# A sliding-window copy by DMA alone: what is staged in SBUF, and how the rest is cut

## The chip, the cores and the metric

The kernel runs on one core of one Trainium2 chip. The metric is the device time of one execution in microseconds; the times given are medians of several runs. The profile is of one more execution, and its span, from the first to the last recorded instruction, lies a little under the timed value.

## What is computed

The reference cuts each of 32 sequences into overlapping windows. It is a pure copy:

```python
x: float32 [32, 4096, 256];  window_size = 64;  stride = 32
n_windows = (4096 - 64) // 32 + 1            # 127
for i in range(n_windows):
    result[:, i] = x[:, i * 32 : i * 32 + 64]
```

With a stride of half a window, each sequence ("batch") is 128 **blocks** of 32 rows, 32 KiB each. Window w is block w followed by block w + 1. So each block but the first and the last of a batch is written twice: as the first half (half 0) of window w, and as the second half (half 1) of window w - 1. The output has 32 x 127 x 2 = 8128 halves of 32 KiB, 266.3 MB; the input has 134.2 MB.

## The kernel before

There are two ways for a block to get to its two places. **Direct**: a DMA from HBM to HBM, which reads the block once for each place. **Staged**: one DMA loads the block into SBUF, two DMAs store it from there. A direct block moves two blocks' worth of bytes through the DMA engines, a staged one three; but a direct block reads HBM twice, a staged one once. The kernel mixes both. SyncE's queue carries the direct copies, ScalarE's the staging, GpSimd's the windows that lie between a staged and a direct batch.

The helpers that name the copies:

```python
DIRECT, IN, OUT = 32768, 16384, 16384        # longest piece of a row, bytes

def windows(self, q, b, w0, n, half=None, piece=DIRECT):
    # n windows of batch b from w0: whole (64 KiB rows) or one half of each (32 KiB rows)
    row = [1, 2 * blk if half is None else blk]
    ...out=self.oap(..., [[2 * blk, n], row]), in_=self.xap(..., [[blk, n], row])...

def load(self, q, t, b, c, rows):            # SBUF tile [128, block] <- blocks, one a partition
def store(self, q, t, b, c, rows, half):     # one half of n windows <- tile
```

Eleven batches of 32 are staged whole, 128 blocks to a tile, in groups of 6 tiles: six loads, twelve stores, and the same for the other five. A load waits for the stores that last used its tile; a store waits for its load.

```python
staged = [*range(1, B, 3)]
items = [(b, -1 if b == B - 1 else 0, c.nb) for b in staged]
...
for g in group: self.load(q, g)      # one DMA of 128 rows (the very first in 4 parts)
for g in group: self.store(q, g)     # two DMAs of 128 rows: half 0, half 1
```

A whole batch of blocks stored at both halves puts one half before the batch's first window and one after its last; these belong to the neighbouring batches, and are written over later.

The direct copies are 16 windows a DMA, either as one DMA of whole windows or as two of halves. How often they are halved depends on what the staging ring is thought to be doing then (`share`):

```python
share += 120 if turns < 16 or -8 <= second < 16 else 90 if loading else 18
if share >= 120:
    share -= 120; turns += 4
    count(c.windows(ring_d, b, w, 16, 0), done)
    count(c.windows(ring_d, b, w, 16, 1), sem)
else:
    turns += 3
    count(c.windows(ring_d, b, w, 16), sem)
```

What 16 doesn't divide, and the windows that staged batches wrote over, come at the end on GpSimd's queue, 15 windows a DMA:

```python
ring_r.wait_ge(near, 16)             # the second-last of the direct copies
for b, w, n in edges:                # wait for the neighbours' stores, then
    count(c.windows(ring_r, b, w, n), rest)
count(c.columns(ring_r, last, 116, 9), rest)     # the last windows in small pieces
st.wait_stored(ring_d, place[B - 1])
count(c.columns(ring_d, last, 125, 2), done)
```

Of the kernel before, what the change touches and what calls it, by code (L numbers as in the profile page):

```python
# [8 lines left out]
DIRECT, IN, OUT = 32768, 16384, 16384  # L9


class Copier:


    def __init__(self, x, out, B, L, D, W, S, n_win):
        assert W == 2 * S and L % S == 0
        self.x, self.out = x, out
        self.B = B
        self.blk = S * D
        self.nb = L // S  # L20
        self.nw = n_win

    def xap(self, block, dims):
        return bass.AP(self.x.tensor, self.x.offset + block * self.blk, dims)

    def oap(self, half_window, dims):
        return bass.AP(self.out.tensor, self.out.offset + half_window * self.blk, dims)

    def windows(self, q, b, w0, n, half=None, piece=DIRECT):

        blk = self.blk
        row = [1, 2 * blk if half is None else blk]
        h = half or 0
        return q.dma_start(  # L34
            out=self.oap((b * self.nw + w0) * 2 + h, [[2 * blk, n], row]),
            in_=self.xap(b * self.nb + w0 + h, [[blk, n], row]),
            max_dma_last_dim=piece,
        )

    def columns(self, q, b, w0, n):  # L40

        part = self.blk // 8
        row = [1, part]
        return q.dma_start(  # L44
            out=self.oap((b * self.nw + w0) * 2, [[part, 16], [2 * self.blk, n], row]),
            in_=self.xap(b * self.nb + w0, [[part, 16], [self.blk, n], row]),
        )

    def load(self, q, t, b, c, rows):

        p, step, n, unit = rows
        return q.dma_start(
            out=t[p : p + (n - 1) * step + 1 : step, :],
            in_=self.xap(b * self.nb + c + p // unit, [[step // unit * self.blk, n], [1, self.blk]]),
            max_dma_last_dim=IN,
        )

    def store(self, q, t, b, c, rows, half):


        p, step, n, unit = rows
        w = b * self.nw + c + p // unit - half
        return q.dma_start(
            out=self.oap(2 * w + half, [[2 * step // unit * self.blk, n], [1, self.blk]]),
            in_=t[p : p + (n - 1) * step + 1 : step, :],
            max_dma_last_dim=OUT,
        )


class Staging:  # L70


    def __init__(self, c, tc, pool, dtype, items, bufs):
        self.c, self.items = c, items
        self.tiles = [pool.tile([128, c.blk], dtype, name=f"xb{i}") for i in range(bufs)]
        self.loaded = [tc.alloc_semaphore(f"loaded{i}") for i in range(bufs)]
        self.stored = [tc.alloc_semaphore(f"stored{i}") for i in range(bufs)]
        self.ended = tc.alloc_semaphore("ended")
        self.count = {sem: 0 for sem in (*self.loaded, *self.stored, self.ended)}
        self.after_load, self.after_store = {}, {}  # L80

    def issue(self, dma, sem):
        dma.then_inc(sem, 16)
# [1 line left out]

    def load(self, q, g):
        i = g % len(self.tiles)
        b, c, n = self.items[g]
        if self.count[self.stored[i]]:
            q.wait_ge(self.stored[i], self.count[self.stored[i]])  # L90
        step = 128 // n
        parts = [(k, 4, 32, 1) for k in range(4)] if g == 0 else [(0, step, n, step)]
        for rows in parts:
            self.issue(self.c.load(q, self.tiles[i], b, c, rows), self.loaded[i])
        self.after_load[g] = self.count[self.loaded[i]]

    def store(self, q, g):
        i = g % len(self.tiles)
        b, c, n = self.items[g]
        q.wait_ge(self.loaded[i], self.after_load[g])  # L100
        step = 128 // n
        parts, end = [((0, step, n, step), 0), ((0, step, n, step), 1)], []
        if g == len(self.items) - 1:

            parts = [((0, 1, 128, 1), 1), ((0, 1, 32, 1), 0)]
            end = [(96, 1, 32, 1)] + [(32 + k, 4, 16, 1) for k in range(4)]
        for rows, half in parts:
            self.issue(self.c.store(q, self.tiles[i], b, c, rows, half), self.stored[i])
        for rows in end:
            self.issue(self.c.store(q, self.tiles[i], b, c, rows, 0), self.ended)  # L110
        self.after_store[g] = self.count[self.stored[i]]

    def wait_stored(self, q, g):
        q.wait_ge(self.stored[g % len(self.tiles)], self.after_store[g])  # L114

    def run(self, q):
        bufs = len(self.tiles)
        for first in range(0, len(self.items), bufs):
            group = range(first, min(first + bufs, len(self.items)))
            for g in group:  # L120
                self.load(q, g)
            for g in group:
                self.store(q, g)


@with_exitstack
def kernel(
    ctx: ExitStack,
    tc: tile.TileContext,
    x: bass.AP,  # L130
    window_size: bass.AP,
    stride: bass.AP,
    out: bass.AP,
):
    nc = tc.nc
    W, S = int(window_size), int(stride)
    B, L, D = x.shape
    n_win = (L - W) // S + 1
    assert out.shape == (B, n_win, W, D)
    c = Copier(x, out, B, L, D, W, S, n_win)  # L140


    staged = [*range(1, B, 3)]
    items = [(b, -1 if b == B - 1 else 0, c.nb) for b in staged]
    place = {b: g for g, (b, _, n) in enumerate(items) if n == c.nb}
    direct = [b for b in range(B) if b not in staged]
    pool = ctx.enter_context(tc.tile_pool(name="xb", bufs=1))
    st = Staging(c, tc, pool, x.dtype, items, 6)
    ring_d, ring_s, ring_r = nc.sync, nc.scalar, nc.gpsimd
    done = tc.alloc_semaphore("done")  # L150
    near = tc.alloc_semaphore("near")
    rest = tc.alloc_semaphore("rest")
    total = {done: 0, near: 0, rest: 0}

    def count(dma, sem):
        dma.then_inc(sem, 16)
        total[sem] += 16

    sixteens = []
    for b in direct:
        w = 15 if b - 1 in staged else 0
        sixteens += [(b, w + 16 * j) for j in range((c.nw - w) // 16)]
    singles = [(B - 1, c.nw - 1, 1)]
    edges = [(b, 0 if b - 1 in staged else 112, 15) for b in direct[:-1]]
    last = B - 2
    edges.append((last, 112, 4))

    first_loads, loads, stores = 6 * 17, 5 * 17, 6 * 34  # L170
    turns = share = 0
    with tc.tile_critical():  # L172
        st.run(ring_s)

        for i, (b, w) in enumerate(sixteens):
            sem = near if i == len(sixteens) - 2 else done
            second = turns - first_loads - stores
            loading = turns < first_loads or 0 <= second < loads
            share += 120 if turns < 16 or -8 <= second < 16 else 90 if loading else 18
            if share >= 120:  # L180
                share -= 120
                turns += 4
                count(c.windows(ring_d, b, w, 16, 0), done)
                count(c.windows(ring_d, b, w, 16, 1), sem)
            else:
                turns += 3
                count(c.windows(ring_d, b, w, 16), sem)
            if i == len(sixteens) // 2:
                for b, w, half in singles:
                    count(c.windows(ring_d, b, w, 1, half, 2048), done)  # L190

        ring_r.wait_ge(near, 16)
        for b, w, n in edges:
            for k in (b - 1, b + 1):
                if k in place and b != last:
                    st.wait_stored(ring_r, place[k])
            count(c.windows(ring_r, b, w, n), rest)


        count(c.columns(ring_r, last, 116, 9), rest)  # L200
        st.wait_stored(ring_d, place[B - 1])
        count(c.columns(ring_d, last, 125, 2), done)
        total[st.ended] = st.count[st.ended]
        for sem, n in total.items():
            ring_d.wait_ge(sem, n)


# [33 lines left out]
```

## Time and profile before

| | |
|---|---|
| time, median of 3 runs | 755.48 us (754.17 to 756.32) |
| span of the profiled execution | 749.4 us |
| bytes through the DMA engines | 313.26 MB, mean 418 GB/s |
| busy engines | GpSimd 12.8 us, for issuing; no other |
| DMAs on SyncE, ScalarE, GpSimd | 204, 41, 22 |

The page's line of tenths shows how busy the core's 16 DMA engines are in 40 equal slices of the span, and the line under it the GB/s they moved. A queue's line has its packets, their bytes, and the time they took as a share of 16 engines' span. A direct copy is counted once in the bytes, though HBM is both read and written; HBM's own traffic stands in a line of its own. Packets under 512 B are those that count up a semaphore at a DMA's end, one on each engine. Sizes of DMAs, and how long one took from issue to landing (the median), are in the last part of the page:

| DMAs | count | KB each | us to landing |
|---|---|---|---|
| direct, whole windows (SyncE) | 92 | 1024 | 100.7 |
| direct, halves (SyncE) | 110 | 512 | 90.3 |
| loads (ScalarE) | 10 | 4096 | 131.4 |
| edges (GpSimd) | 20 | 960 | 38.5 |

A load or a store of a whole tile is 128 rows of 32 KiB, 4096 KB. Landing times are long because the queues are deep.

### The profile page before, as it was taken

The numbers are of one execution on the slowest core, as the hardware profiler recorded it, in microseconds if no ns is written. First come the engines' busy times: TensorE is split into PE (matmuls) and PEld (weight loads), VectorE is DVE, ScalarE is ACT, GpSimd is POOL, SyncE is SP. The second block draws the span as 40 slices with busy tenths as digits, with TensorE's granted clock in tenths as the row PEclk, the third lists the DMA queues.
The fourth block names the chain that finished last, engine by engine and source line by source line (L and its number), as shares of the span: only waits on it lengthen the run. The fifth ranks groups of instructions, "written<-read, shape, count | busy, mean of one in ns | idle before, by whom it ended". The sixth has DMA issues, their size and how long they took to land.

```text
span 749.4 us, 322 instructions
## 1 busy us (share of the span) xinstructions
POOL 12.8 (2%) x26
## 2 busy tenths in 40 slices
POOL 0000000000000000000000000000000000040100
DMA  8999999999999999999999999999999999999996
GB/s 360 401 427 429 427 429 428 434 423 418 420 424 423 418 424 415 422 427 427 414 427 417 429 432 429 430 422 430 429 423 421 423 421 419 425 426 423 431 409 262
DMA packets 18290, 313.26 MB, mean 418 GB/s; under 512 B 4336, under 2 KB 4336, under 8 KB 4528
## 3 DMA queue, kind: packets, MB, share of 16 engines
q1 hardware_dynamic: 8016, 154.32, 48.8%
q10 hardware_dynamic: 9104, 138.41, 44.0%
q0 software_dynamic: 1168, 20.51, 6.5%
q14 instruction: 2, 0.02, 0.0%
HBM read 220.95 MB, written 267.09 MB: 651 GB/s over the span
## 4 chain that ended last, share of the span: by engine, by line
another core or an unknown queue 92%; POOL 2%; issue 0%; POOLq 0%; SPq 0%
POOL out_dram L34 2%; POOL out_dram L44 0%; POOLq L236 0%; SPq L172 0%; POOLq L114 0%
## 5 line engine op out<-in xcount | busy, mean ns | idle before, releaser
L34 POOL DMA_DIRECT2D out_dram<-in_x_dram x21 | 12.0, 576 | 691.3 <-DMA out_dram<-in_x_dram 654.0
L44 POOL DMA_DIRECT2D out_dram<-in_x_dram x1 | 0.6, 581 | 0.0
L222 POOL MEMSET const-float32-0.0<- 128x1 f32 x1 | 0.1, 98 | 0.2 <-issue 0.2
L222 POOL MEMSET const-bfloat16-1.0<- 128x1 bf16 x1 | 0.1, 101 | 0.0
L222 POOL MEMSET const-float32-1.0<- 128x1 f32 x1 | 0.1, 98 | 0.0
L222 POOL MEMSET const-uint8-127<- 128x1 uint8 x1 | 0.1, 98 | 0.0
## 6 DMA issues: line engine op xcount, KB each, us to landing
out_dram<-in_x_dram SPq DMA_DIRECT2D x92, 1024.0 KB, 100.7
out_dram<-xb ACTq DMA_DIRECT2D x21, 4096.0 KB, 139.7
out_dram<-in_x_dram SPq DMA_DIRECT2D x110, 512.0 KB, 90.3
xb<-in_x_dram ACTq DMA_DIRECT2D x10, 4096.0 KB, 131.4
out_dram<-in_x_dram POOLq DMA_DIRECT2D x20, 960.0 KB, 38.5
xb<-in_x_dram ACTq DMA_DIRECT2D x4, 1024.0 KB, 15.7
out_dram<-xb ACTq DMA_DIRECT2D x2, 1024.0 KB, 113.4
out_dram<-xb ACTq DMA_DIRECT2D x4, 512.0 KB, 96.9
```

What stands on the lines that cost most here:

```text
L34: return q.dma_start(out=self.oap((b * self.nw + w0) * 2 + h, [[2 * blk, n], row]), in_=self.xap(b * self.nb + w0 + h, [[blk, n], row]), m ...
L44: return q.dma_start(out=self.oap((b * self.nw + w0) * 2, [[part, 16], [2 * self.blk, n], row]), in_=self.xap(b * self.nb + w0, [[part, 16 ...
L222: nc = _bacc.Bacc("TRN2", target_bir_lowering=False, num_devices=1)
```

## The change

It changes what is staged. Instead of all 128 blocks of 11 batches, the inner blocks 1 to 64 of 23 batches are: each of them belongs in two windows of its own batch, so nothing is stored outside its place. Two batches, 16 apart, share a tile: one has the even partitions, the other the odd ones; each has its own load and its own two stores of 64 rows. Batch 11 has a tile alone.

```diff
-    staged = [*range(1, B, 3)]
-    items = [(b, -1 if b == B - 1 else 0, c.nb) for b in staged]
+    far, pairs, n = B // 2, 11, 64
+    items = [(g, far, 1, n) for g in range(pairs + 1)]
+    alone = pairs
```

```diff
-        step = 128 // n
-        parts = [(k, 4, 32, 1) for k in range(4)] if g == 0 else [(0, step, n, step)]
+        step = 4 if g == 0 else 2
+        for k in range(step if g != self.alone else 1):
+            dma = self.c.load(q, self.tiles[i], b + far * (k % 2), c + k // 2, k, step, 2 * n // step)
```

```diff
+        for half in (0, 1):
+            for k in (0, 1) if g != self.alone else (0,):
+                self.issue(self.c.store(q, self.tiles[i], b + far * k, c, k, n, half), self.stored[i])
```

The direct copies follow from it. Windows 65 to 112 of every batch go 16 a DMA (`whole`). The nine batches that aren't staged have their blocks 1 to 64 copied as halves (`split`). Windows 113 to 126 don't make a sixteen; these are gathered **across** 16 batches, one window of each in a DMA, so the rows read lie a whole batch (4 MiB) apart. The same goes for the two halves that border on the staged part (half 0 of window 0, half 1 of window 64).

```diff
+    def across(self, q, b, w, half=None):
+            out=self.oap(b, w, h, [[2 * self.nw * blk, 16], row]),
+            in_=self.xap(b, w + h, [[self.nb * blk, 16], row]),
...
+    for b in range(B):
+        whole += [(b, w) for w in range(n + 1, n + 49, 16)]
+        if b % far >= pairs and b != alone:
+            split += [(b, w) for w in range(0, n, 16)]
+    for w in range(n + 49, n_win):
+        cross += [(b, w) for b in (0, far)]
+    where = len(whole) // 4
+    jobs = whole[:where] + cross + whole[where:]          # shortened
```

The balance between the rings is set anew, with many more halves; a halved turn takes a split pair first, while there are any:

```diff
-    first_loads, loads, stores = 6 * 17, 5 * 17, 6 * 34
+    first_loads, loads, stores = 6 * 18, 5 * 18 + 9, 6 * 36
...
-            share += 120 if turns < 16 or -8 <= second < 16 else 90 if loading else 18
+            share += 120 if turns < 16 or -8 <= second < 16 else 106 if loading else 95
```

GpSimd's queue, the edges, the small pieces at the end (`columns`) and the waits for neighbours' stores are gone; SyncE waits for its own copies and for all stores.

```diff
-        ring_r.wait_ge(near, 16)
-        for b, w, n in edges:
-            ...
-        count(c.columns(ring_r, last, 116, 9), rest)
-        st.wait_stored(ring_d, place[B - 1])
-        count(c.columns(ring_d, last, 125, 2), done)
+        ring_d.wait_ge(done, total)
+        st.wait_all(ring_d)
```

## The prediction

> **What bounds the kernel now.** No engine computes; all is transfers. So the first view to read is the page's second and third parts: how busy the 16 DMA engines are, and what each queue moved.
>
> ```profile
> DMA  8999999999999999999999999999999999999996
> GB/s 360 401 427 429 427 429 428 434 423 418 420 424 423 418 424 415 422 427 427 414 427 417 429 432 429 430 422 430 429 423 421 423 421 419 425 426 423 431 409 262
> DMA packets 18290, 313.26 MB, mean 418 GB/s; under 512 B 4336, under 2 KB 4336, under 8 KB 4528
> ...
> q1 hardware_dynamic: 8016, 154.32, 48.8%
> q10 hardware_dynamic: 9104, 138.41, 44.0%
> q0 software_dynamic: 1168, 20.51, 6.5%
> ...
> HBM read 220.95 MB, written 267.09 MB: 651 GB/s over the span
> ```
>
> The DMA engines are full in every slice but the first and the last. q1 is SyncE's ring (direct copies, 32 KiB pieces), q10 ScalarE's (staging, 16 KiB pieces), q0 GpSimd's (the edges). There is no gap to close in the middle, so the time is bytes through the engines divided by a rate, plus what is lost at the two ends. The second view, the table of stretches, shows that this rate isn't one number:
>
> ```profile
> 0.00:20.00 20.00, 0.20 (x4) 1.00 0.90 367
> 20.00:40.00 20.00, 0.00 (x0) 1.00 1.00 401
> ...
> 200.00:300.00 100.00, 0.00 (x0) 1.00 1.01 421
> ...
> 440.00:540.00 100.00, 0.00 (x0) 1.00 1.01 429
> 560.00:640.00 80.00, 0.00 (x0) 1.00 1.01 423
> 660.00:740.00 80.00, 6.95 (x13) 1.00 1.01 421
> 740.00:749.00 9.00, 0.00 (x0) 1.00 0.31 127
> ```
>
> The last column is GB/s, the one before it the DMA engines' busy share. The rate moves between 421 and 429 with the engines equally full. The third view, the queues in two of these stretches, says with what it moves. From 200 to 300 us, then from 440 to 540 us:
>
> ```profile
> q1 hardware_dynamic: 1173, 24.18, 57.6%
> q10 hardware_dynamic: 1176, 17.96, 42.9%
> ```
>
> ```profile
> q1 hardware_dynamic: 1275, 23.30, 54.5%
> q10 hardware_dynamic: 1274, 19.56, 46.1%
> ```
>
> A direct byte crosses HBM twice, a staged one once. In the first stretch 24.18 / 42.14 MB = 57.4% of the bytes are direct, at 421 GB/s; in the second 23.30 / 42.86 = 54.4%, at 429 GB/s. From 560 to 640 us it is again 57% (19.40 of 33.81 MB), at 423. In HBM traffic that is 421 x 1.574 = 663 GB/s against 429 x 1.544 = 662: about the same. So I read two limits that lie close together: the engines' own rate (near 430) and HBM's (near 663), and a mix with more direct bytes falls to the second. The waits view confirms that nothing but ring ends is waited for: GpSimd's 654 us are the wait, by design, for the second-last direct copy.
>
> ```profile
> POOL out_dram L34 <- DMA out_dram<-in_x_dram: 654.0, 1, 654.0
> POOL out_dram L34 <- DMA out_dram<-xb: 37.4, 1, 37.4
> ```
>
> **What the Trainium skill says.** (1) "DMA: Bandwidth & Descriptors", section "Where 436 GB/s comes from": 16 ports of 32 B at 850 MHz make 435 GB/s. The trace agrees: its best long stretch has 429. (2) The same page, "Queues, rings and completion order": each engine takes the queue rows it has work for in turn, a packet of each. The trace agrees closely: 1173 to 1176 packets and 1275 to 1274 in the stretches above. So a ring's share of the bytes follows from its packets' sizes, the 4-byte semaphore packets counting as turns too. (3) "HBM Reference", "Specifications (TRN2)": about 716 GB/s for the domain. 663 GB/s is 93% of that, near enough to call it a limit that is felt. (4) The first page again, "Latency and other measured facts": copies whose rows lie 4 MiB apart in both tensors ran at half rate (103 against 214 GB/s a direction), rows 512 KiB apart at full rate. No stretch of this trace has such a pitch; the change brings one.
>
> **The change, part by part.**
>
> *Bytes.* Staged loads: before 11 batches x 128 blocks = 1408 blocks, after 23 x 64 = 1472. Blocks are 32 KiB, so loads go from 46.14 to 48.23 MB, +2.10 MB. The halves that whole-batch staging stored outside their place (one at each end of 11 batches, 22 of 32 KiB, 0.72 MB) go. After: the output's 8128 window halves of 32 KiB, 266.34 MB, plus 48.23 MB of loads make 314.57 MB, against 313.26 on the page. At the mean middle rate of before, 424 GB/s, +1.31 MB is **+3.1 us**.
>
> *The mix.* Of the 8128 halves 2944 come from the staging tiles, 5184 are direct: 169.87 MB, 54.0% of 314.57. Before it was 154.32 + 20.51 = 174.83 MB, 55.8%. And the changed schedule spreads it evenly: SyncE's DMAs are nearly all halves (two packets for 32 KiB) throughout, where before the loading stretches had many halves and the storing stretches few. From the instruction order, 28 whole copies and 268 halves remain, 324 data and 296 semaphore packets an engine, 620 turns. Staging makes 552 data packets and 71 semaphores, 623 turns. Taking turns, both rings run from start to end, and every stretch should have 53 to 56% direct, like the stretch at 429. I take 428.5 GB/s: 314.57 MB / 428.5 = 734.1 us. Before, the middle from 40 to 740 us ran at 424 (313.26 less 7.34, 8.02 and 1.14 MB in 700 us); at that rate the new bytes would take 741.9. The mix is thus worth **-7.8 us**. As a cross-check, packet times from the 440 to 540 stretch: 46.1% of 1600 us over 1194 packets of 16 KiB is 0.618 us, 54.5% over 711 of 32 KiB is 1.226 us. 552 x 0.618 + 324 x 1.226 = 738 engine-us, and as the shares there add to 1.006, 734 us of time.
>
> *The ends.* The first 40 us moved 15.36 MB instead of 17.1 at 428.5, a loss of 4.1 us. The new start (the same four-part first tile, the same halves) keeps it. The last 9.4 us moved 1.14 MB, a loss of 6.7 us. Of that, the part owed to GpSimd's late edges, 15 windows on 16 engines, may go; but the 16 engines still finish apart, and the small columns that evened them out are gone as well. I keep 6.5.
>
> *More DMAs.* 267 become 367 (71 on ScalarE, 296 on SyncE, none on GpSimd), so 100 more 4-byte packets an engine. The stretch with most of them (644 of 2549) is the fastest, so I take 0 to 1 us: 0.5. Issue is no limit: SyncE's shortest took 0.57 us, 296 x 0.57 = 169 us.
>
> *Across 16 batches.* 28 copies of 1 MiB and 4 of 512 KiB read rows 4 MiB apart, one row on each engine; by the turns they run at about 275 to 400 us. The skill's slow case has 128 rows, so on 16 engines of 8 consecutive rows the engines stand 8 pitches apart (an estimate from that page): 32 MiB where it was slow, 4 MiB where the 512 KiB pitch was fast. Here engines stand 4 MiB apart, and only the reads. I charge 2 us.
>
> *Half-tile staging DMAs.* Loads and stores now take every second partition, 64 rows. The first tile's parts (32 rows, every fourth partition) did already: from 3 to 8 us q10 had 1.03 MB at 52.7%, 42 us over 63 packets, 0.67 us each, at a cold start, against 0.618. No cost is charged.
>
> Sum: 734.1 + 4.1 + 6.5 + 0.5 + 2 = 747.2 us of span, against 749.4. The timed median lies 6.1 above the span before (755.48); with the same added, **753 us**.
>
> **Rivals.** *Only bytes count*: if the engines' 424 is a fixed mean and the mix tells nothing, the time is 755.5 + 3 = 758 to 759. For it: engines are equally "full" at 421 and 429. Against: the rate follows the direct share in three stretches. *HBM rows collide*: if the 4 MiB pitch halves the cross copies' rate, their 60 to 62 packets of 1.23 us an engine take 75 us more, about 825; a tenth of that effect gives 760. Against it: engines drift apart, and the other ring's packets lie between; no row of before can show it. *The rings come apart*: if one ring ends early, the other runs alone; were it the direct one, all its bytes would cross HBM twice and 663 / 2 = 331 GB/s remain, so 10 us of overhang cost about 3. The turns (620 and 623) speak against more. *The end shrinks*: without GpSimd's edges the tail could lose 3 us less, giving 750.
>
> **Range and chances.** 753 is the sum; 745 needs the mix, no pitch cost and a better end; 764 holds the bytes-only case with some pitch cost. Over 2% faster would be under 740.4, which needs the engines' best rate in every stretch and no lost ends: 4%. Over 2% slower is above 770.6, the pitch rival at a fifth of its size or more: 9%. Within 2%: 87%.
>
> **What would show it.** Right: about 314.6 MB, HBM read 218 MB, no q0; stretches from 40 to 730 us at 427 to 430 with 53 to 56% direct; q1 and q10 both busy to the last 10 us. Wrong: a dip of GB/s between 275 and 400 us with full engines (the pitch); 424 at 54% direct (the mix tells nothing); q10 packets above 0.63 us (the half tiles); a last stretch with one queue alone. The pitch is what would make it most wrong.

## The result and the profile after

The changed kernel took **812.28 us** (median of 6 runs, 810.13 to 815.88), against 755.66 for the kernel before in the same set: 1.0754 times as long, 95% interval 1.0725 to 1.0782. The prediction had 753, within 745 to 764.

The page of the changed kernel, the lines that answer to those shown of before:

```profile
DMA  8999999999999999999999999999999999999996
GB/s 363 422 425 410 432 430 424 432 430 426 428 422 426 374 269 287 297 283 265 293 291 276 319 429 428 401 426 424 431 429 428 420 426 425 427 422 429 421 424 292
DMA packets 19891, 314.62 MB, mean 388 GB/s; under 512 B 5872, under 2 KB 5872, under 8 KB 5872
...
q1 hardware_dynamic: 9920, 169.89, 53.9%
q10 hardware_dynamic: 9968, 144.71, 45.6%
...
HBM read 218.10 MB, written 266.34 MB: 597 GB/s over the span
```

The bytes are as counted, and the DMA engines are "busy" throughout. The row of tenths alone would show nothing wrong. The row under it does: from the 14th slice to the 23rd the rate is about a third lower, and on both sides of that it is the old one. The table of stretches (busy share of the DMA engines, then GB/s, at the end of each line; the last line is the clean stretch behind the dip):

```profile
200.00:250.00 50.00, 0.00 (x0) 1.00 1.00 425
250.00:300.00 50.00, 0.00 (x0) 1.00 1.02 356
300.00:350.00 50.00, 0.00 (x0) 1.00 1.00 285
350.00:400.00 50.00, 0.00 (x0) 1.00 1.01 285
400.00:450.00 50.00, 0.00 (x0) 1.00 1.00 283
450.00:500.00 50.00, 0.00 (x0) 1.00 1.01 395
...
550.00:790.00 240.00, 0.00 (x0) 1.00 1.01 426
```

That is where the copies across 16 batches run. The five stretches from 250 to 500 us moved 50 us x (356 + 285 + 285 + 283 + 395) = 80.2 MB, which takes 188 us at the 426 GB/s of the stretch from 550 to 790 us: **62 us** are lost there. Without them the span of 811.5 would be about 749.5.

How the loss looks to each queue: SyncE's (q1) and ScalarE's (q10), first from 300 to 450 us, then from 600 to 700 us, each line with packets, MB and the share of 16 engines' time:

```profile
q1 hardware_dynamic: 1348, 23.14, 54.7%
q10 hardware_dynamic: 1347, 19.48, 45.8%
```

```profile
q1 hardware_dynamic: 1332, 23.10, 54.6%
q10 hardware_dynamic: 1333, 19.37, 45.9%
```

The packets, the MB and the shares are nearly equal; only the stretches differ, 150 us and 100. A direct piece of 32 KiB took 54.7% x 2400 us / 706 = 1.86 us instead of 54.6% x 1600 / 705 = 1.24. And a staged piece of 16 KiB, which has nothing to do with the across copies but runs on the same engines and HBM, took 0.92 instead of 0.62. Of the across copies an engine has 56 pieces, and by the ratio of the stretch (706 to 1189) some 94 staged ones beside them: 56 x 0.62 + 94 x 0.30 = 63 us, the loss again.

### The profile page after: what moved, and what is told of

The parts are those of the page before. It is cut to its first block, busy times and chain, and to the rows that moved or that the text cites. A ratio compares the mean times of both kernels' runs of the same rounds, so it can differ in the third digit from the quotient of the medians.

```text
span 811.5 us, 420 instructions
## 1 busy us (share of the span) xinstructions
POOL 0.2 (0%) x4
## 2 busy tenths in 40 slices
DMA packets 19891, 314.62 MB, mean 388 GB/s; under 512 B 5872, under 2 KB 5872, under 8 KB 5872
## 3 DMA queue, kind: packets, MB, share of 16 engines
HBM read 218.10 MB, written 266.34 MB: 597 GB/s over the span
```

## The experiments

The sets below ran on different chips; the kernel before took 745 to 756 us on them, so each ratio is against the kernel before on the same chip, and rates in GB/s are best compared within a run or on one chip. Theory A is that rows a multiple of 4 MiB apart, read by 16 engines at once, are slow. Theory B is that gathering from 16 far batches is slow whatever the pitch, or that the far writes are.

### Another pitch for the reads alone

```diff
-            in_=self.xap(b, w + h, [[self.nb * blk, 16], row]),
+            in_=self.xap(b, w + h - 15, [[(self.nb + 1) * blk, 16], row]) if w > self.nb // 2
+            else self.xap(b, w + h, [[self.nb * blk, 16], row]),
```

> The across copies read rows 4 MiB + 32 KiB apart instead of 4 MiB (so they read other blocks than the reference asks for); the writes, sizes, counts and order are as in the changed kernel. Theory A (the reads' exact 4 MiB pitch slows them): the dip of 283 to 285 GB/s goes, every stretch has 425 to 430, and the time falls from 812 to 747 to 755 us. Theory B (writes 127 windows apart, or gathering from 16 batches at whatever pitch): the dip stays, about 812 us. If the pitch were only part of it, something between.

752.33 us, 1.0012 times the kernel before (0.9997 to 1.0026). The across copies' stretch, then the clean one after it, from the table of stretches of this run:

```profile
280.00:410.00 130.00, 0.00 (x0) 1.00 1.01 415
480.00:730.00 250.00, 0.00 (x0) 1.00 1.01 429
```

415 instead of 285: the reads' pitch is what costs. The same far batches, writes and counts are there, so theory B falls. The remaining 14 GB/s over 130 us are 4 us. The rate was expected at 425 or more, so the time came out as theory A had it and the stretch a little short. (This kernel copies other blocks to windows 113 to 126 than the reference asks for; so do the next two and the last one.)

### Four pitches in one run

```diff
+    for i, pitch in enumerate([4194304, 2097152, 1048576, 524288]):
+        jobs += [("whole", *k) for k in whole[24 * i : 24 * i + 12]]
+        jobs += [(pitch // 4, *k) for k in cross[7 * i : 7 * i + 7]]
+        jobs += [("whole", *k) for k in whole[24 * i + 12 : 24 * i + 24]]
```

> The 28 across copies in four groups of 7, apart from each other in the order, with reads at a pitch of 4 MiB, 2 MiB, 1 MiB and 512 KiB (other blocks than the reference asks for; same writes). Theory A: the first group dips to about 285 GB/s for some 45 us, the second to between 285 and 428, the last two not below 420; the time is about 812 - 63 x 3/4 + a part for 2 MiB, 765 to 785 us. Theory B: four equal dips, about 812 us in all.

771.7 us, one run. Each group's stretch was found from its copies' issue and their 88 us to landing. The table of stretches, 4 MiB, 2 MiB, 1 MiB and 512 KiB in order:

```profile
240.00:250.00 10.00, 0.00 (x0) 1.00 1.02 285
...
382.00:412.00 30.00, 0.00 (x0) 1.00 1.01 374
...
540.00:570.00 30.00, 0.00 (x0) 1.00 1.00 396
...
682.00:714.00 32.00, 0.00 (x0) 1.00 1.00 413
```

The first line is the bottom of its dip, 10 us; from 226 to 262 us the mean is 295. The cost falls with each halving, and a trace of it is left at 512 KiB (the stretches between have 424 to 429). The last two were expected at 420 or more; neither gets there.

### The same pitch with a few KiB more

The diff is that of the run before, with the pitches 4 MiB + 4, + 16, + 64 and + 128 KiB.

> Again four groups of 7 across copies, with reads at 4 MiB + 4 KiB, + 16 KiB, + 64 KiB and + 128 KiB (other blocks than the reference asks for; same writes). If what matters is that the 16 engines read at addresses that agree in their low bits, a few KiB of offset from row to row mends it: the first group is slow or half mended (300 to 400 GB/s), the other three have 410 or more, as the + 32 KiB pitch had (415). If far rows as such are slow, all four are at 290 to 400.

759.73 us, one run, on a chip where the kernel before takes 745.49. The four groups in order:

```profile
226.00:256.00 30.00, 0.00 (x0) 1.00 1.01 298
380.00:410.00 30.00, 0.00 (x0) 1.00 0.99 394
...
530.00:560.00 30.00, 0.00 (x0) 1.00 1.00 428
670.00:700.00 30.00, 0.00 (x0) 1.00 1.02 434
```

So in this run 16 batches far apart cost nothing once 64 KiB are added to the 4 MiB from one row to the next. 16 KiB mend most of it, less than expected (410 or more), and 4 KiB next to nothing: the 16 engines then stand within 60 KiB of each other modulo 4 MiB, which is two of the pieces they copy. That this is a matter of channels or banks of HBM is a likely reading, but nothing here shows it.

### The writes

```diff
-    def across(self, q, b, w, half=None):
+    def across(self, q, b, w, half=None, skew=1):
...
-            out=self.oap(b, w, h, [[2 * self.nw * blk, 16], row]),
-            in_=self.xap(b, w + h, [[self.nb * blk, 16], row]),
+            out=self.oap(b, w, h, [[2 * (self.nw + skew) * blk, 16], row]),
+            in_=self.xap(b, w + h, [[(self.nb + skew) * blk, 16], row]),
```

> The across copies step one window further with each batch, so that they read 4 MiB + 32 KiB apart and write exactly 8 MiB apart (both sides of the same window, so what is copied is right); to make room 16 windows of each batch are left out (33.6 MB less is written). If writes suffer from such a pitch as reads do, the stretch of the across copies falls to about 290 GB/s; if only reads do, it stays above 410. The whole time isn't compared.

The border copies keep `skew=0`. The across copies' stretch and the clean one behind it, from the table of stretches of this one run:

```profile
250.00:400.00 150.00, 0.00 (x0) 1.00 1.01 300
...
460.00:640.00 180.00, 0.00 (x0) 1.00 1.01 431
```

Writes suffer as reads do: reads at 4 MiB + 32 KiB alone had 415. In the changed kernel the writes were spared because the output has 127 windows a batch, not 128, so that its rows are 8 MiB less 64 KiB apart. With these same writes the run before had 428 and 434 GB/s.

### The across copies spread out

```diff
-    jobs += [("cross", *k) for k in cross]
-    jobs += [("whole", *k) for k in whole[where:]]
+    for i, job in enumerate(whole):
+        jobs.append(("whole", *job))
+        if (i + 1) * len(cross) // len(whole) > i * len(cross) // len(whole):
+            jobs.append(("cross", *cross[i * len(cross) // len(whole)]))
```

> The same across copies with their 4 MiB pitch, but one after each three or four of the direct copies of 16 neighbouring windows, instead of 28 in a row. All of the output is computed. If the slow thing is a crowd (all 16 engines at such rows at once, for copy after copy), spreading lets the engines' drift hide most of it: 750 to 770 us, no stretch below 400. If each across copy pays its price by itself, the 63 us stay: 805 to 820 us, with the loss spread evenly over the stretches where they stand (about 380 to 390 GB/s).

780.31 us, 1.0373 times the kernel before (1.0349 to 1.0398). Both expectations miss. The loss is halved and spread: 425 GB/s from 40 to 150 us, 402 to 412 from there on. This fits a cost that is partly the crowd's, copy after copy, and partly each copy's own; no run separates the two further.

### Without across copies: GpSimd's queue again

```diff
-    jobs += [("cross", *k) for k in cross]
...
+        nc.gpsimd.wait_ge(near, 16)
+        for b in range(B):
+            c.windows(nc.gpsimd, b, n + 49, n=n_win - n - 49).then_inc(rest, 16)
```

> No across copies for windows 113 to 126: GpSimd's queue copies these 14 windows of each batch with one DMA a batch, once SyncE's ring is nearly done, as the kernel before did with its edges. The staging of 64 blocks of 23 batches and the even mix stay. All of the output is computed. My sum without a pitch cost gives a span of 745, so about 751 us timed; theory A says 748 to 756. If the staging in half tiles or the larger number of DMAs cost anything of their own, it stays above 760.

754.60 us, 1.0035 (1.0019 to 1.0050), and in a later set 756.49, 1.0019 (1.0011 to 1.0027). With the 28 across copies the changed kernel's loss is gone; the new staging has no cost of its own of that size, but no gain either. Two smaller losses are seen in its stretches: the four border copies, still 4 MiB apart (373 GB/s for 20 us), and GpSimd's whole windows at the end (416 GB/s, with 23.43 of 41.63 MB direct, 56%).

```profile
380.00:400.00 20.00, 0.00 (x0) 1.00 1.01 373
...
640.00:740.00 100.00, 0.00 (x0) 1.00 1.00 416
```

That later set profiled the kernel before beside it on the same chip, to see if the even mix shows:

> The kernel before once more, for a profile from the same chip as the run beside it. If the mix sets the rate, its middle (40 to 700 us) is slower than that of the kernel with the even mix by 3 to 5 GB/s, 1%, and it is its storing stretches that are (by 5 to 8 GB/s against its loading ones). If the gain from the even mix was an accident of one chip, both middles are alike.

> The kernel with the new staging and GpSimd's 14 whole windows once more, on the same chip as the kernel before: again 1.002 to 1.005 times it. The middle up to 600 us at 427 to 431 GB/s, but for the 20 us of the border copies; then about 416 to 427, as more of the bytes are direct there.

From 150 to 250 us the kernel before, storing, had 58% direct bytes at 419 GB/s, the other 54% at 427. But from 40 to 700 us they had 422 and 423, so the expected 3 to 5 GB/s between the middles did not show. Slower in the new kernel were the start (421 GB/s from 40 to 100 us, against 429) and the border copies (367 from 380 to 410 us); GpSimd's ends are alike (416 to 418 from 640 to 740 us, against 415 to 421).

### The border copies removed as well, and the mix by itself

```diff
+    def columns(self, q, w, half):     # 2 KiB columns, one an engine, of one half in all 32 batches
+            out=self.oap(0, w, half, [[part, 16], [2 * self.nw * self.blk, self.B], row]),
+            in_=self.xap(0, w + half, [[part, 16], [self.nb * self.blk, self.B], row]),
...
-            c.windows(nc.gpsimd, b, n + 49, n=n_win - n - 49).then_inc(rest, 16)
+            for half in (0, 1):
+                c.windows(nc.gpsimd, b, n + 49, half, n_win - n - 49).then_inc(rest, 16)
+        c.columns(nc.gpsimd, 0, 0).then_inc(rest, 16)
```

> All of the output is computed, with no row of any DMA a multiple of 4 MiB from the next on another engine: GpSimd's 14 windows a batch as two DMAs of halves, and the two halves that border on the staged part cut into 2 KiB columns, at the ends of GpSimd's and ScalarE's queues. The stretch at 416 GB/s with 56% direct bytes (GpSimd's whole windows) should rise to 427, worth 100 us x 11/428 = 2.6 us, and the dip near 390 us (373 GB/s for 20 us) go, worth another 2.6 us: 749 to 751 us against 752.0 and 754.6 for the kernel with whole windows. If the even mix were worth nothing, 752 or more.

761.49 us, 1.0211 (1.0192 to 1.0229): a miss, as 749 to 751 had been reckoned against 752.0 on the earlier chip. The dip of the border copies is gone (425 GB/s from 380 to 410 us), but see the busy share (second last column) towards the end, from the table of stretches:

```profile
685.00:735.00 50.00, 0.00 (x0) 1.00 0.88 374
735.00:759.00 24.00, 0.00 (x0) 1.00 0.47 146
```

0.88 is 14 of 16. A DMA of 14 single-piece rows seems to have used the same 14 engines every time, so that two had less to do; which engine a packet ran on is not recorded. The next run but one puts the shape of these DMAs to the test. The variant with SyncE's old share in the storing stretches, all else and all bytes equal:

```diff
-            share += 120 if turns < 16 or -8 <= second < 16 else 106 if loading else 95
+            share += 120 if turns < 16 or -8 <= second < 16 else 106 if loading else 18
```

> The kernel without a 4 MiB pitch, with one number changed: SyncE halves few of its copies while the staging ring stores (18 of 120 as in the kernel before, instead of 95), so that direct bytes are some 57% there and the ring of staging is left alone, or nearly, at the end. The same bytes in all. If the mix of a stretch sets its rate, these stretches have 420 to 423 instead of 428, and the time is 3 to 6 us longer than the even one's. If only bytes count, no difference.

765.67 us against 761.49, 4.2 us more. The storing stretch of each, the uneven one first:

```profile
120.00:400.00 280.00, 0.00 (x0) 1.00 1.01 423
```

```profile
120.00:380.00 260.00, 0.00 (x0) 1.00 1.01 431
```

58.5% of the bytes were direct in the first (64.46 of 110.10 MB from 120 to 380 us), 54.3% in the second. This is the mix step of the prediction with the bytes held equal: the stretch with more direct bytes is the slower one. The edit also makes fewer and larger copies, which comes with the mix here, and the size of the effect is not the same everywhere: GpSimd's whole windows had 416 GB/s with 56% direct above, and 427 with 57% (24.22 of 42.72 MB) in the next run, on another chip.

### GpSimd's windows whole again, and the rows of an engine

```diff
-            for half in (0, 1):
-                c.windows(nc.gpsimd, b, n + 49, half, n_win - n - 49).then_inc(rest, 16)
+            c.windows(nc.gpsimd, b, n + 49, n=n_win - n - 49).then_inc(rest, 16)
...
-            share += 120 if turns < 16 or -8 <= second < 16 else 106 if loading else 95
+            share += 120 if turns < 16 or -8 <= second < 16 else 106 if loading else 105
```

The second change, a few more halved copies on SyncE's queue while the staging stores, was made along with the first.

> All of the output is computed. GpSimd copies its 14 windows of a batch whole again, one DMA a batch; the border halves stay cut into columns at the ends of two queues. If the last 85 us of the run before this, with its DMA engines at 0.88, were short of work on two engines of 16 because a DMA of 14 rows in single packets uses the same 14 engines each time, the engines are full again to the end, and the time is about 1.000 times that of the kernel before (0.997 to 1.002): the kernel with 14 whole windows had 1.0035, and the dip of the four border copies, 2.6 us or 0.0035, is gone. If the columns were to blame, it stays at 1.01 or more.

749.92 us, 1.0069 (1.0056 to 1.0082): again a miss, 4.3 us slower than the kernel before. The DMA engines are full while GpSimd's windows run, as they were in the kernel with whole windows and 95 in place of 105, so the shape of GpSimd's DMAs was the larger part of the loss. The end shows where time still goes:

```profile
620.00:720.00 100.00, 0.00 (x0) 1.00 1.01 427
720.00:735.00 15.00, 0.00 (x0) 1.00 1.00 344
735.00:746.00 11.00, 0.00 (x0) 1.00 0.38 117
```

In the last two stretches the columns run. They put all 16 engines within one 32 KiB block, with batches 4 MiB apart: closer than the + 4 KiB rows that were slow. That this is what slows them is argued, not tried; their small pieces are a rival that no run tests. No version that beats the kernel before was found.

The last run asked how rows fall on engines, as the prediction had assumed something about it:

```diff
+        return q.dma_start(
+            out=self.oap(0, w, h, [[2 * self.nw * blk, 32], [1, blk]]),
+            in_=bass.AP(self.x.tensor, self.x.offset + (w + h) * blk, [[pitch, 32], [1, blk]]),
```

> The across copies as DMAs of 32 rows of 32 KiB, two rows an engine: 14 of them with reads 2 MiB apart, then 14 with reads 512 KiB apart (other blocks than the reference asks for). My estimate in the prediction took it that an engine has consecutive rows. If so, the engines stand 4 MiB apart in the first group, which then falls to about 290 to 316 GB/s as the 4 MiB pitch did, and 1 MiB apart in the second (396 on the earlier chip). If row after row goes to engine after engine, the first group has what the 2 MiB pitch had (371 to 395), the second 413.

345 GB/s in the first group (285 to 335 us), 410 in the second. The first lies between the two answers, so the run doesn't decide it. Nor is the comparison clean: these copies were not halved, and 60% of the bytes were direct in both stretches (10.29 of 17.24 MB and 14.71 of 24.60 MB) instead of 54%, which lowers the rate by itself.

## Why the prediction was wrong

**The step that failed is "Across 16 batches".** It charged 2 us, and 62 were lost; a time over 2% slower was given 9%. The Trainium skill's "DMA: Bandwidth & Descriptors", section "Latency and other measured facts", gave the warning, and the prediction named it. It was then argued away: the page's slow case was taken to have engines 32 MiB apart, its fast one 4 MiB, and only the reads were at that pitch here. The runs show that one row an engine at exactly 4 MiB, in the reads alone, brings the stretch to 285 GB/s. Whether an engine has 8 consecutive rows, as its estimate took it, stays open; wrong was the conclusion that engines 4 MiB apart, in the reads only, cost next to nothing. The rival "HBM rows collide" named the right cause, the 4 MiB pitch (where in HBM rows would collide is not shown), and nearly the right size: 75 us, from 61 pieces at double time. Measured was half as much more time a piece (1.24 to 1.86 us), but on the staged pieces between them too. (Over 2% took about a quarter of those 75 us, 770.6 less 751, not a fifth.) The prediction held against it that engines drift apart and that the other ring's packets lie between. That the first can't help much is inferred from the + 4 KiB group, where 60 KiB between the first and the last engine didn't help; the others were slowed themselves. The page's remedy of 4 KiB a row was for 128 rows, by estimate an offset of 512 KiB in all. Here 16 rows with it had 298 GB/s, and it took 64 KiB a row, 960 KiB in all.

**The mix** was right in mechanism and too large in size. The clean stretches of the changed kernel had 54.2% direct (55.32 of 102.12 MB from 550 to 790 us), as foreseen, but 426 GB/s and not 428.5: 314.57 MB / 426 = 738.4 us, so -3.5 us against the 741.9 at before's rate, not -7.8. The rate had been taken from the best 100 us of one run. In the test above the mix was worth 4.2 us. Such a gain about pays for the 3.1 us of added bytes, which fits that the kernels without the 28 slow copies end level with the kernel before or a little above it. Nor is HBM's 663 GB/s a fixed limit: the two stretches of GpSimd's whole windows come to 416 x 1.563 = 650 and 427 x 1.567 = 669.

**What held**: the bytes (314.62 MB; HBM read 218.10); no queue for GpSimd; no cost of half tiles (0.62 us a piece, as before); the rings' ends (both still move bytes from 795 us on). The ends cost as charged: the first 40 us 15.8 MB, 3 us short (4.1 foreseen), the last 11.5 us 2.2 MB, 6.3 short (6.5 foreseen). With 738.4, 3, 6.3 and 0.5 the sum is 748 us, and 62 more make 810, near the span of 811.5.

## What to carry to other kernels

A full DMA row in the profile says only that engines hold packets; look at GB/s beside it, and at the time a packet takes. When 16 rows of one DMA lie a large power of two apart, on either side, move them by some 64 KiB a row, as helped here, or cut the work along another axis before anything else is tuned. And a measured warning that fits the case should widen the range until a run has ruled it out: an argument about how its geometry differs is not a measurement.

## What was not expected of the hardware

- The slow rows slow their neighbours: ScalarE's staged pieces went from 0.62 to 0.92 us beside them.
- The cost is graded: 285 GB/s at 4 MiB, 374 at 2 MiB, 396 at 1 MiB, 413 at 512 KiB; 298, 394, 428 and 434 with 4, 16, 64 and 128 KiB added to 4 MiB, on another chip.
- GpSimd's DMAs of 14 rows in one piece each left the engines 0.88 busy; the same rows in two pieces each left them 1.00 busy.
